# Rotary embedding on one core: the first and last rows as f32 on SyncE's queue, a new order of partitions, and constants copied by a shuffle

## The chip, the core and the metric

One core of a Trainium2 chip runs the whole program. Times are device microseconds (us); lower is better. "Span" is the stretch that the profile covers, from the program's first to its last profiled instruction; the time of an execution is a little longer. GpSimd, SyncE and ScalarE each issue transfers on a queue of their own (q0, q1 and q10 in the pages); the core's 16 DMA engines move them in packets. A transfer has *landed* when all 16 of its completions are in the records. A *drain* is an instruction that waits until its engine's work is done. f32 numbers take 4 bytes, bf16 numbers 2. The verdict "faster" or "slower" needs 2%.

## The reference

Every row of 64 numbers is rotated by an angle that depends on its position in the sequence (0 to 1023) and on the column.

```python
batch, n_heads, seq, head_dim = 8, 8, 1024, 64      # x is f32: 16.8 MB in, 16.8 MB out
angles = np.outer(positions, freqs)                 # freqs has 32 entries
cos, sin = np.cos(angles), np.sin(angles)
out_first  = x_first * cos - x_second * sin
out_second = x_first * sin + x_second * cos
```

## The kernel before

The 64 (batch, head) pairs make 8 tiles of 8 heads. A partition holds a chunk of 64 consecutive rows of one head: 16 KB in f32, 8 KB as bf16 on the chip. GpSimd issues all loads and stores of x and out; they cast between f32 and bf16. ScalarE makes the sines once; VectorE does six multiplies or adds for each tile.

```python
    def hbm(t, g):
        return bass.AP(tensor=t.tensor, offset=t.offset + g * P * run, ap=[[run, P], [1, run]])

    pos_i = singles.tile([P, C, 1], positions.dtype)
    nc.sync.dma_start(                                  # each of 128 partitions reads its 512 B
        out=pos_i,
        in_=bass.AP(tensor=positions.tensor, offset=positions.offset,
                    ap=[[0, group], [C, chunks], [1, C]]))
    fr = singles.tile([P, half], f32)
    nc.scalar.dma_start(out=fr, in_=freqs[None, :].to_broadcast([P, half]))   # 128 x 128 B

    for g in range(ntiles):
        xt = xpool.tile([P, C, d], bf16)
        nc.gpsimd.dma_start(out=xt.rearrange("p c d -> p (c d)"), in_=hbm(x, g))
    # ... turns on VectorE, then sin_h and cos_h on ScalarE (cut) ...
    for g in range(ntiles):
        # ... six operations on VectorE, 128x2048 bf16 each (cut) ...
        nc.gpsimd.dma_start(out=hbm(out, g), in_=ot.rearrange("p c d -> p (c d)"))
```

Of the kernel before, what the change touches and what calls it, by code (L numbers as in the profile page):

```python
# [2 lines left out]

# [4 lines left out]


@with_exitstack  # L10
def kernel(
    ctx: ExitStack,
    tc: tile.TileContext,
    x: bass.AP,
    freqs: bass.AP,
    positions: bass.AP,
    out: bass.AP,
):
    nc = tc.nc
    f32 = mybir.dt.float32  # L20
    bf16 = mybir.dt.bfloat16
    Sin = mybir.ActivationFunctionType.Sin
    Alu = mybir.AluOpType

    b, h, seq, d = x.shape
    bh = b * h
    half = d // 2
    P = 128
    twopi = 2 * math.pi


    C = 64
    chunks = seq // C
    group = P // chunks
    ntiles = bh // group
    run = C * d
    assert chunks * C == seq and group * chunks == P and ntiles * group == bh

    singles = ctx.enter_context(tc.tile_pool(name="singles", bufs=1))
    xpool = ctx.enter_context(tc.tile_pool(name="xin", bufs=ntiles))  # L40
    opool = ctx.enter_context(tc.tile_pool(name="xout", bufs=ntiles))
    tpool = ctx.enter_context(tc.tile_pool(name="tmp", bufs=2))

    def hbm(t, g):
        return bass.AP(tensor=t.tensor, offset=t.offset + g * P * run, ap=[[run, P], [1, run]])


    pos_i = singles.tile([P, C, 1], positions.dtype)
    nc.sync.dma_start(
        out=pos_i,  # L50
        in_=bass.AP(tensor=positions.tensor, offset=positions.offset,
                    ap=[[0, group], [C, chunks], [1, C]]))
    fr = singles.tile([P, half], f32)
    nc.scalar.dma_start(out=fr, in_=freqs[None, :].to_broadcast([P, half]))


    xts = []
    for g in range(ntiles):
        xt = xpool.tile([P, C, d], bf16)
        nc.gpsimd.dma_start(out=xt.rearrange("p c d -> p (c d)"), in_=hbm(x, g))  # L60
        xts.append(xt)


    half_pi = singles.tile([P, 1], f32)
    nc.vector.memset(half_pi, math.pi / 2)  # L65
    pos_f = singles.tile([P, C, 1], f32)
    nc.vector.tensor_copy(out=pos_f, in_=pos_i.bitcast(mybir.dt.int32)[:, :, :1])  # L67
    fturn = singles.tile([P, 1, half], f32)
    nc.vector.tensor_scalar_mul(out=fturn[:, 0, :], in0=fr, scalar1=1.0 / twopi)  # L69
    turns = singles.tile([P, C, half], f32)  # L70
    nc.vector.tensor_mul(out=turns, in0=pos_f.to_broadcast([P, C, half]),  # L71
                         in1=fturn.to_broadcast([P, C, half]))
    whole = singles.tile([P, C, half], f32)
    magic = 1.5 * 2.0 ** 23
    nc.vector.tensor_scalar(out=whole, in0=turns, scalar1=magic, scalar2=magic,  # L75
                            op0=Alu.add, op1=Alu.subtract)
    nc.vector.tensor_sub(out=turns, in0=turns, in1=whole)  # L77
    sin_h = singles.tile([P, C, half], bf16)
    cos_h = singles.tile([P, C, half], bf16)
    nc.scalar.activation(out=sin_h, in_=turns, func=Sin, scale=twopi)  # L80

    nc.scalar.activation(out=whole, in_=turns, func=mybir.ActivationFunctionType.Abs)  # L82
    nc.scalar.activation(out=cos_h, in_=whole, func=Sin, scale=-twopi, bias=half_pi)  # L83

    v = nc.vector
    for g in range(ntiles):
        xt = xts[g]
        xf = xt[:, :, :half]
        xs = xt[:, :, half:]
        ot = opool.tile([P, C, d], bf16)  # L90
        of = ot[:, :, :half]
        os_ = ot[:, :, half:]
        t1 = tpool.tile([P, C, half], bf16)
        t2 = tpool.tile([P, C, half], bf16)
        v.tensor_mul(out=t1, in0=xf, in1=sin_h)  # L95
        v.tensor_mul(out=t2, in0=xs, in1=sin_h)  # L96
        v.tensor_mul(out=of, in0=xf, in1=cos_h)  # L97
        v.tensor_mul(out=os_, in0=xs, in1=cos_h)  # L98
        v.tensor_sub(out=of, in0=of, in1=t2)  # L99
        v.tensor_add(out=os_, in0=os_, in1=t1)  # L100
        nc.gpsimd.dma_start(out=hbm(out, g), in_=ot.rearrange("p c d -> p (c d)"))  # L101


# [1 line left out]
_INS = ['x', 'freqs', 'positions']  # L105
_OUTS = [((8, 8, 1024, 64), 'float32')]


# [23 lines left out]
```

## Time and profile before

| | before |
|---|---|
| time, median of 4 runs | 86.48 us (86.45 to 86.63) |
| profiled run: time, span | 86.43, 84.25 us |
| last load landed (tile 7) | 43.93 us |
| VectorE's last result | 67.7 us |
| last packet / last landing of a store | 82.46 / 82.83 us |
| from the last landing to the end of the span | 1.41 us |

The page of the kernel before: the span; the busy share of two rows in 40 equal slices, in tenths; then for each DMA queue its packets, MB and the share of 16 engines' span.

```profile
span 84.2 us, 132 instructions
DVE 60.7 (72%) x54; ACT 7.0 (8%) x4; POOL 8.9 (11%) x20
...
DVE  0069927999999999999999999999999910000000
...
DMA  0399999999999999999999999999999999999990
...
q0 software_dynamic: 2304, 25.17, 97.2%
q1 hardware_dynamic: 136, 0.07, 0.3%
q10 hardware_dynamic: 144, 0.02, 0.1%
```

The DMA engines are full from the third slice to the last but one. VectorE (DVE) has nothing to do in the last seven slices, so its speed does not matter here. In the packet records an engine moves a row of 16 KB (f32 side) every 0.605 us, in loads and in stores, so 16 engines move 433 GB/s and x and out together need 77.5 us. Only the rest can be won.

The start, in stretches of 0.5 us (stretch, its length, busy us and instructions of VectorE, ScalarE and GpSimd, clock, DMA share, GB/s):

```profile
2.00:2.50 0.50, 0.00 (x0) 0.42 (x1) 0.50 (x2) 1.00 0.20 52
2.50:3.00 0.50, 0.00 (x0) 0.00 (x0) 0.50 (x2) 1.00 0.44 52
3.00:3.50 0.50, 0.00 (x0) 0.00 (x0) 0.50 (x2) 1.00 0.37 38
3.50:4.00 0.50, 0.00 (x0) 0.00 (x0) 0.50 (x3) 1.00 0.44 70
4.00:4.50 0.50, 0.00 (x0) 0.00 (x0) 0.50 (x2) 1.00 0.98 221
```

When all 16 engines are full, they move about 215 GB/s by this count, because a load is counted by its bf16 bytes. Until 4 us there is almost nothing. GpSimd issues its first load at 1.25 us, yet the first sixteen packets of its queue start at 2.8 to 4.5 us.

The end, in SyncE's own waits (who waited for what: total us, times, longest):

```profile
SPq L127 <- DMA out_dram<-ot: 81.2, 4, 66.8
SPq L127 <- PEq L127: 1.0, 2, 0.6
```

SyncE waits for the stores nearly all the time. The last one lands at 82.83 us, and SyncE is through at 83.11; but in the instruction records GpSimd's closing drain ends only at 83.53 us, 0.70 us after the landing, and the closing barriers come after that.

### The profile page before, as it was taken

Reading aid. Unit: us, or ns where it says so; the run is one execution under the profiler, and the core shown is the slowest. Engines: PE = TensorE matmul, PEld = TensorE weight load, DVE = VectorE, ACT = ScalarE, POOL = GpSimd, SP = SyncE. Lnnn points to the kernel's source line nnn. Section 1 sums busy time; section 2 is a strip of 40 time slices with the busy share of each in tenths; the row PEclk is TensorE's granted clock in tenths of the full one; section 3 lists DMA queues with packets and bytes.
Section 4 is the critical chain, followed back from the end, with each engine's and each line's share of the span. In section 5 each row is a group of like instructions: output and inputs, shape, how many; then the busy total and the mean of one; then the engine's idle time right before and its main releaser. Section 6 shows DMA issues by size and latency. Waiting matters only on the chain.

```text
span 84.2 us, 132 instructions
## 1 busy us (share of the span) xinstructions
DVE 60.7 (72%) x54; ACT 7.0 (8%) x4; POOL 8.9 (11%) x20
## 2 busy tenths in 40 slices
DVE  0069927999999999999999999999999910000000
ACT  4100079900000000000000000000000000000000
POOL 5960000000201100200200200100020020000000
DMA  0399999999999999999999999999999999999990
GB/s 2 60 210 214 214 218 218 214 214 214 214 222 210 218 218 210 218 218 214 210 342 405 459 405 467 381 490 381 482 389 467 405 451 420 428 443 405 467 373 0
DMA packets 2584, 25.25 MB, mean 300 GB/s; under 512 B 408, under 2 KB 536, under 8 KB 536
## 3 DMA queue, kind: packets, MB, share of 16 engines
q0 software_dynamic: 2304, 25.17, 97.2%
q1 hardware_dynamic: 136, 0.07, 0.3%
q10 hardware_dynamic: 144, 0.02, 0.1%
HBM read 16.86 MB, written 16.78 MB: 399 GB/s over the span
## 4 chain that ended last, share of the span: by engine, by line
issue 65%; DMA 10%; POOL 4%; POOLq 1%; PEldq 0%
DMA xt<-in_x_dram 10%; POOL out_dram L101 4%; POOLq L127 1%; POOLq L101 0%; PEldq L127 0%
## 5 line engine op out<-in xcount | busy, mean ns | idle before, releaser
L95 DVE TENSOR_TENSOR t<-xt,sin_h 128x2048 bf16<-128x2048 bf16 x8 | 9.8, 1224 | 2.0 <-ACT sin_h L80 2.0
L101 POOL DMA_DIRECT2D out_dram<-ot x8 | 4.3, 535 | 58.6 <-DVE ot L100 58.6
L99 DVE TENSOR_TENSOR ot<-ot,t 128x2048 bf16<-128x2048 bf16 x8 | 9.8, 1225 | 0.0
L97 DVE TENSOR_TENSOR ot<-xt,cos_h 128x2048 bf16<-128x2048 bf16 x8 | 9.8, 1224 | 0.0
L100 DVE TENSOR_TENSOR ot<-ot,t 128x2048 bf16<-128x2048 bf16 x8 | 9.8, 1224 | 0.0
L98 DVE TENSOR_TENSOR ot<-xt,cos_h 128x2048 bf16<-128x2048 bf16 x8 | 9.8, 1223 | 0.0
L96 DVE TENSOR_TENSOR t<-xt,sin_h 128x2048 bf16<-128x2048 bf16 x8 | 9.8, 1223 | 0.0
L60 POOL DMA_DIRECT2D xt<-in_x_dram x8 | 4.4, 578 | 0.8 <-PEq L127 0.8
L67 DVE CAST pos_f<-pos_i 128x64 f32<-128x64 int32 x1 | 0.2, 196 | 4.1 <-DMA pos_i<-in_positions_dram 4.1
L80 ACT ACTIVATE sin_h<-turns 128x2048 bf16<-128x2048 f32 x1 | 1.9, 1911 | 8.7 <-DVE turns L77 8.7
L77 DVE TENSOR_TENSOR turns<-turns,whole 128x2048 f32<-128x2048 f32 x1 | 2.3, 2293 | 0.0
L71 DVE TENSOR_TENSOR turns<-pos_f,fturn 128x2048 f32<-128x2048 f32 x1 | 2.3, 2291 | 0.0
L83 ACT ACTIVATE cos_h<-whole,half_pi 128x2048 bf16<-128x2048 f32 x1 | 2.0, 2003 | 0.0
L82 ACT ACTIVATE whole<-turns 128x2048 f32<-128x2048 f32 x1 | 1.9, 1896 | 0.0
L80 ACT ACT_TABLE_LOAD x1 | 1.3, 1283 | 1.1 <-PEq L116 1.1
L75 DVE TENSOR_SCALAR whole<-turns 128x2048 f32<-128x2048 f32 x1 | 1.2, 1226 | 0.0
L65 DVE MEMSET half_pi<- 128x1 f32 x1 | 0.1, 59 | 0.8 <-PEq L116 0.8
L69 DVE TENSOR_SCALAR fturn<-fr 128x32 f32<-128x32 f32 x1 | 0.2, 174 | 0.0
L116 POOL MEMSET const-float32-0.0<- 128x1 f32 x1 | 0.1, 99 | 0.2 <-issue 0.2
L116 POOL MEMSET const-bfloat16-1.0<- 128x1 bf16 x1 | 0.1, 102 | 0.0
L116 POOL MEMSET const-float32-1.0<- 128x1 f32 x1 | 0.1, 99 | 0.0
L116 POOL MEMSET const-uint8-127<- 128x1 uint8 x1 | 0.1, 99 | 0.0
## 6 DMA issues: line engine op xcount, KB each, us to landing
out_dram<-ot POOLq DMA_DIRECT2D x8, 2048.0 KB, 21.7
xt<-in_x_dram POOLq DMA_DIRECT2D x8, 1024.0 KB, 23.6
pos_i<-in_positions_dram SPq DMA_DIRECT2D x1, 64.0 KB
fr<-in_freqs_dram ACTq DMA_DIRECT2D x1, 16.0 KB, 3.6
```

The lines of the kernel that those rows point to most:

```text
L60: nc.gpsimd.dma_start(out=xt.rearrange("p c d -> p (c d)"), in_=hbm(x, g))
L71: nc.vector.tensor_mul(out=turns, in0=pos_f.to_broadcast([P, C, half]), in1=fturn.to_broadcast([P, C, half]))
L77: nc.vector.tensor_sub(out=turns, in0=turns, in1=whole)
L80: nc.scalar.activation(out=sin_h, in_=turns, func=Sin, scale=twopi)
L83: nc.scalar.activation(out=cos_h, in_=whole, func=Sin, scale=-twopi, bias=half_pi)
L95: v.tensor_mul(out=t1, in0=xf, in1=sin_h)
L96: v.tensor_mul(out=t2, in0=xs, in1=sin_h)
L97: v.tensor_mul(out=of, in0=xf, in1=cos_h)
L98: v.tensor_mul(out=os_, in0=xs, in1=cos_h)
L99: v.tensor_sub(out=of, in0=of, in1=t2)
L100: v.tensor_add(out=os_, in0=os_, in1=t1)
L101: nc.gpsimd.dma_start(out=hbm(out, g), in_=ot.rearrange("p c d -> p (c d)"))
```

## The change

The intent: let SyncE's queue carry f32 rows while GpSimd's queue is not yet, or no longer, the bottleneck, and read less at the start. The first 16 of 64 rows of each partition of tile 0 come in as f32 in two pieces of 8 rows (2 KB runs), and ScalarE casts them. The last 24 rows of tile 7 are computed in f32 and go out on SyncE in three such pieces. A partition now holds chunk p//8 of head p%8, so that one copy of the positions for every 8 partitions and one of the frequencies for every 32 are enough; VectorE's shuffle copies them within groups of 32. SyncE waits for the earlier transfers before the end instead of at the end. Tile 1 is rotated before tile 0.

```diff
+    def hbm(t, g, lo=0, hi=C):
+        return bass.AP(tensor=t.tensor, offset=t.offset + g * P * run + lo * d,
+                       ap=[[run, chunks], [seq * d, group], [1, (hi - lo) * d]])
+    piece = 8
+    head = 2 * piece
+    x0 = singles.tile([P, head, d], f32)
+    for r in range(0, head, piece):
+        nc.sync.dma_start(out=x0[:, r:r + piece], in_=hbm(x, 0, r, r + piece))
+    nc.vector.memset(pos_i, 0)
+    nc.scalar.dma_start(out=pos_i[0:P:group].bitcast(positions.dtype), in_=...)  # 16 rows
+    nc.vector.memset(fr, 0.0)
+    nc.scalar.dma_start(out=fr[0:P:32], in_=freqs[None, :].to_broadcast([P // 32, half]))
     for g in range(ntiles):
+        lo = 0 if g else head
+        nc.gpsimd.dma_start(out=xts[g][:, lo:], in_=hbm(x, g, lo))
+    nc.vector.stream_shuffle(pos_i, pos_i, [i // group * group for i in range(32)])
+    nc.vector.stream_shuffle(fr, fr, [0] * 32)
 ...
+    nc.scalar.copy(out=xts[0][:, :head], in_=x0)
+    tail = 3 * piece
+    for g in [1, 0] + list(range(2, ntiles)):
+        hi = C if g < ntiles - 1 else C - tail
 ...
+    last = singles.tile([P, tail, d], f32)
+    rotate(ntiles - 1, C - tail, C, last)
+    sp.keepalive_nop(ins=[sp.lower_ap(cos_h)])
+    for done in [pos_i, fr, x0] + ots[:-1]:
+        sp.clobber_nop(outs=[sp.lower_ap(done)])       # SyncE waits here, before the end
+    for r in range(0, tail, piece):
+        ... sp.dma_start(out=hbm(out, ntiles - 1, lo, lo + piece), in_=last[:, r:r + piece])
+    sp.clobber_nop(outs=[sp.lower_ap(ots[-1])])
```

More of the change, by code (lines that the diff above doesn't have):

```diff
@@ L42 @@
     tpool = ctx.enter_context(tc.tile_pool(name="tmp", bufs=2))
-    def hbm(t, g):
-        return bass.AP(tensor=t.tensor, offset=t.offset + g * P * run, ap=[[run, P], [1, run]])
-    pos_i = singles.tile([P, C, 1], positions.dtype)
-    nc.sync.dma_start(
-        out=pos_i,
+    def hbm(t, g, lo=0, hi=C):
+        return bass.AP(tensor=t.tensor, offset=t.offset + g * P * run + lo * d,
+                       ap=[[run, chunks], [seq * d, group], [1, (hi - lo) * d]])
+    xts = [xpool.tile([P, C, d], bf16, name="xt") for _ in range(ntiles)]
+    piece = 8
[3 more added lines that the diff above has]
+        nc.sync.dma_start(out=x0[:, r:r + piece], in_=hbm(x, 0, r, r + piece))
+    i32 = mybir.dt.int32
+    words = mybir.dt.size(positions.dtype) // 4
+    pos_i = singles.tile([P, C, words], i32)
+    nc.vector.memset(pos_i, 0)
+    nc.scalar.dma_start(
+        out=pos_i[0:P:group].bitcast(positions.dtype),
         in_=bass.AP(tensor=positions.tensor, offset=positions.offset,
-                    ap=[[0, group], [C, chunks], [1, C]]))
+                    ap=[[C, chunks], [1, C], [1, 1]]))
     fr = singles.tile([P, half], f32)
-    nc.scalar.dma_start(out=fr, in_=freqs[None, :].to_broadcast([P, half]))
-    xts = []
+    nc.vector.memset(fr, 0.0)
+    nc.scalar.dma_start(out=fr[0:P:32], in_=freqs[None, :].to_broadcast([P // 32, half]))
     for g in range(ntiles):
-        xt = xpool.tile([P, C, d], bf16)
-        nc.gpsimd.dma_start(out=xt.rearrange("p c d -> p (c d)"), in_=hbm(x, g))
-        xts.append(xt)
+        lo = 0 if g else head
+        nc.gpsimd.dma_start(out=xts[g][:, lo:], in_=hbm(x, g, lo))
+    nc.vector.stream_shuffle(pos_i, pos_i, [i // group * group for i in range(32)])
+    nc.vector.stream_shuffle(fr, fr, [0] * 32)
     half_pi = singles.tile([P, 1], f32)
@@ L66 @@
     pos_f = singles.tile([P, C, 1], f32)
-    nc.vector.tensor_copy(out=pos_f, in_=pos_i.bitcast(mybir.dt.int32)[:, :, :1])
+    nc.vector.tensor_copy(out=pos_f, in_=pos_i[:, :, :1])
     fturn = singles.tile([P, 1, half], f32)
@@ L83, with rotate @@
     nc.scalar.activation(out=cos_h, in_=whole, func=Sin, scale=-twopi, bias=half_pi)
+    nc.scalar.copy(out=xts[0][:, :head], in_=x0)
     v = nc.vector
-    for g in range(ntiles):
-        xt = xts[g]
-        xf = xt[:, :, :half]
-        xs = xt[:, :, half:]
-        ot = opool.tile([P, C, d], bf16)
+    def rotate(g, lo, hi, ot):
+        xf = xts[g][:, lo:hi, :half]
+        xs = xts[g][:, lo:hi, half:]
         of = ot[:, :, :half]
         os_ = ot[:, :, half:]
-        t1 = tpool.tile([P, C, half], bf16)
-        t2 = tpool.tile([P, C, half], bf16)
-        v.tensor_mul(out=t1, in0=xf, in1=sin_h)
-        v.tensor_mul(out=t2, in0=xs, in1=sin_h)
-        v.tensor_mul(out=of, in0=xf, in1=cos_h)
-        v.tensor_mul(out=os_, in0=xs, in1=cos_h)
+        sin = sin_h[:, lo:hi]
+        cos = cos_h[:, lo:hi]
+        t1 = tpool.tile([P, C, half], bf16, name="t1")[:, :hi - lo]
+        t2 = tpool.tile([P, C, half], bf16, name="t2")[:, :hi - lo]
+        v.tensor_mul(out=t1, in0=xf, in1=sin)
+        v.tensor_mul(out=t2, in0=xs, in1=sin)
+        v.tensor_mul(out=of, in0=xf, in1=cos)
+        v.tensor_mul(out=os_, in0=xs, in1=cos)
         v.tensor_sub(out=of, in0=of, in1=t2)
         v.tensor_add(out=os_, in0=os_, in1=t1)
-        nc.gpsimd.dma_start(out=hbm(out, g), in_=ot.rearrange("p c d -> p (c d)"))
+    tail = 3 * piece
+    ots = []
+    for g in [1, 0] + list(range(2, ntiles)):
+        hi = C if g < ntiles - 1 else C - tail
+        ot = opool.tile([P, C, d], bf16, name="ot")[:, :hi]
+        rotate(g, 0, hi, ot)
+        ots.append(ot)
+        nc.gpsimd.dma_start(out=hbm(out, g, 0, hi), in_=ot)
+    last = singles.tile([P, tail, d], f32)
+    rotate(ntiles - 1, C - tail, C, last)
+    sp = nc.sync
+    sp.keepalive_nop(ins=[sp.lower_ap(cos_h)])
+    for done in [pos_i, fr, x0] + ots[:-1]:
+        sp.clobber_nop(outs=[sp.lower_ap(done)])
+    for r in range(0, tail, piece):
+        lo = C - tail + r
+        tc.keep_in_program_order(
+            sp.dma_start(out=hbm(out, ntiles - 1, lo, lo + piece), in_=last[:, r:r + piece]))
+    sp.clobber_nop(outs=[sp.lower_ap(ots[-1])])
+    for r in range(0, tail - piece, piece):
+        sp.clobber_nop(outs=[sp.lower_ap(last[:, r:r + piece])])
 _INS = ['x', 'freqs', 'positions']
```

## The prediction

> **What bounds the kernel now.** The DMA engines. The page's slices show DMA at 9 (90% or more) from the third slice to the last but one; the software queue takes 97.2% of 16 engines' span. Stretches: loads run at 214 to 216 GB/s counted on the bf16 side (about 430 in f32) from 4 to 43 us, stores at 418 to 440 GB/s until 82 us. VectorE is 72% busy and off the path: a store queued at 22.6 us (timeline) only moves after the loads, at 43 us, and VectorE ends at 68 us, 14 us before the DMA. In the packet records one engine moves a 16 KB f32 row every 0.605 us, so 128 rows cost 77.5 us. The rest, 84.2 - 77.5 = 6.7 us, is start and end; only that can be won.
>
> *Start.* GpSimd issues the first load at 1.25 us; its packets start between 2.8 and 4.5 us; the engines are full from about 4.7 us. From 0 to 4 us the DMA share is 0.18, mostly constants (q1, q10: 0.4% of 16 engines' span; q1's packets of 27 ns, on 8 engines only, sit at 2.2 to 4.5 us, among the first loads).
>
> *End.* The last packet is at 82.4 us, the last landing at 82.83 us. GpSimd's closing drain ends only at 83.53 us, 0.7 us later; closing barriers follow to 84.2. SyncE is through its waits at 83.1 us, so GpSimd's drain sets the end.
>
> **What the change does.**
> 1. 16 of 64 rows of tile 0 (32 KB an engine) leave GpSimd's queue: 2 x 0.605 = 1.21 us of transfer. Issued at 0.74 us on SyncE, they should flow from about 1.8 to 2.3 us (the constants' packets began 1.0 and 1.5 us after their issue), mostly while the engines idle. The Trainium skill ("DMA: Bandwidth & Descriptors", Issuing engines are not separate DMA queues) says all queues share the 16 engines; so this gains only where they idle now. Gain 1.0 to 1.2 us.
> 2. Constants: 128 + 128 rows become about 16 + 4. Gain 0.1 to 0.4 us on the engines that finish last. Two shuffles and two memsets on VectorE (some 0.1 to 0.2 us each): off the path.
> 3. The tail on SyncE: same bytes, so no transfer gain; 24 packets of 2 KB an engine may cost 0.1 to 0.3 us more. But GpSimd's queue finishes about 1 us before the end, so its 0.7 us drain hides, and SyncE's earlier waits are done beforehand: gain 0.5 to 0.6 us.
> 4. f32 outputs of 24 rows put tile 7 on VectorE at about 10 instead of 7 us, the cast of tile 0 about 1 us on ScalarE: within the 14 us of slack.
> 5. The new order of partitions changes the HBM stride; I expect the same 0.605 us.
>
> Sum: about 1.1 + 0.25 + 0.55 - 0.15 = 1.75 us, or a little more, of 86.46.
>
> **Prediction:** 84.6 us, 83.6 to 85.5 in 8 of 10. Faster by over 2% 0.58, within 2% 0.39, slower 0.03.
>
> **What would show each step:** x0 packets between 1.8 and 4 us, tile 0's and tile 1's landings about 1.2 us earlier; loads ending near 41.8 us; SyncE's queue last to land, near 81.4 us; SyncE's drain and not GpSimd's last before the closing barrier, the span ending 0.85 us after the landing rather than 1.4; VectorE ending near 71 to 72 us.
>
> **What would make it wrong:** x0's small packets come so slowly that they collide with GpSimd's first loads; the tail's three issues on SyncE come late and leave the engines idle (they wait for tile 6's landing first); the new stride slows HBM.

## The result

| | before | after |
|---|---|---|
| time, median of 4 runs | 86.48 | 85.36 us (85.36 to 85.53) |
| ratio after / before | | 0.9872 (0.9855 to 0.9889) |
| profiled run: time, span | 86.43, 84.25 | 85.36, 83.58 |
| time outside the span | 2.19 | 1.78 |
| tile 1 landed / tile 7 landed | 14.67 / 43.93 | 13.96 / 43.24 |
| tile 6 stored: 15 engines / the last | 77.97 / 77.98 | 77.26 / 77.77 |
| last landing | 82.83 | 82.69 |
| last landing to end of span | 1.41 | 0.89 |

A ratio is the mean time of one kernel's fast runs over that of the other's fast runs of the same rounds, so it is not quite the ratio of the medians. The change is 1.3% faster: within 2%, and inside the range that was predicted, but the gain is 1.1 us where 1.75 or a little more was summed.

The page after, the lines that answer to those of before:

```profile
span 83.6 us, 163 instructions
DVE 63.5 (76%) x66; ACT 9.3 (11%) x6; POOL 8.7 (10%) x20
...
DVE  1024995089999999999999999999999999920000
...
DMA  0899999999999999999999999999999999999992
...
q0 software_dynamic: 2304, 24.12, 94.2%
q1 hardware_dynamic: 720, 1.31, 5.1%
q10 hardware_dynamic: 40, 0.01, 0.0%
q14 instruction: 1, 0.01, 0.0%
```

The last line is new: one packet that fetches instructions. It becomes important. The start after:

```profile
2.00:2.50 0.50, 0.00 (x0) 0.00 (x0) 0.50 (x2) 1.00 0.51 102
2.50:3.00 0.50, 0.00 (x0) 0.00 (x0) 0.50 (x2) 1.00 0.91 156
3.00:3.50 0.50, 0.00 (x0) 0.00 (x0) 0.50 (x2) 1.00 0.77 140
3.50:4.00 0.50, 0.00 (x0) 0.00 (x0) 0.50 (x2) 1.00 1.26 325
4.00:4.50 0.50, 0.00 (x0) 0.00 (x0) 0.50 (x2) 1.00 1.09 223
```

The engines are busy 1.5 us earlier than before, yet the loads land only 0.7 us earlier. SyncE's waits after, and its issue of the tail (start, length, what):

```profile
SPq L137 <- DMA out_dram<-ot: 56.7, 7, 27.1
...
SPq L144 <- DMA out_dram<-last: 1.9, 2, 1.3
...
SPq L170 <- DMA out_dram<-last: 0.5, 1, 0.5
```

```profile
77.84 2.27 SPq L141 DMA_DIRECT2D out_dram<-last  x3
```

At the end only one wait, for the last piece, is left. GpSimd's drain ends at 81.50 us, before the last landing, and SyncE's at 82.83.

The difference of the two profiled runs, 1.07 us, in parts: the start -0.71 (tile 1, tile 7 and 15 of 16 engines at tile 6 all agree within 0.02 us); from there to the last landing 0.57 is given back (-0.71 becomes -0.14); the closing part -0.52; the time outside the span -0.41.

**A measure used below.** *Lag* at time t is t minus the time that the bytes of x and out moved by then would take at 433 GB/s (packet records, f32 side: a bf16 load packet counts twice). Constants do not count. A smaller lag is better; where lag grows, the engines lose time there.

| kernel | lag at 5 | 12 | 40 | 44 | 77 us | last landing | closing | outside |
|---|---|---|---|---|---|---|---|---|
| before | 4.24 | 4.40 | 4.56 | 4.67 | 4.78 | 82.83 | 1.41 | 2.19 |
| after | 3.28 | 3.64 | 3.80 | 3.91 | 4.10 | 82.69 | 0.89 | 1.78 |
| e1 head only | 3.55 | 4.37 | 4.53 | 4.55 | 4.66 | 82.93 | 1.42 | 2.21 |
| e2 order and constants only | 3.16 | 3.31 | 3.51 | 4.63 | 4.78 | 83.18 | 1.42 | 1.78 |
| e3 tail only | 4.46 | 4.62 | 4.78 | 4.81 | 4.95 | 83.54 | 0.86 | 1.77 |
| e4 after, 8 early rows | 3.39 | 3.51 | 3.68 | 3.99 | 4.18 | 82.67 | 0.88 | 1.80 |
| e5 before, 8 memsets | 4.42 | 4.57 | 4.74 | 4.75 | 4.91 | 83.54 | 1.41 | 1.77 |
| e6 after, 46 memsets | 3.26 | 3.62 | 3.81 | 3.90 | 4.05 | 82.45 | 0.88 | 1.79 |
| e7 after, no early rows | 3.29 | 3.40 | 3.56 | 4.60 | 4.75 | 83.39 | 0.85 | 1.78 |
| e8 after, no tail | 3.31 | 3.59 | 3.75 | 3.83 | 4.01 | 82.36 | 1.43 | 1.79 |
| e9 order only | 3.89 | 4.10 | 4.26 | 4.54 | 4.65 | 82.76 | 1.42 | 2.20 |
| e10 constants only, old order | 3.82 | 3.92 | 4.08 | 4.37 | 4.54 | 83.04 | 1.44 | 1.77 |
| e11 e10 with the tail | 3.83 | 3.92 | 4.08 | 4.32 | 4.49 | 83.10 | 0.89 | 1.78 |
| e12 e11, 46 memsets | 3.85 | 3.95 | 4.14 | 4.25 | 4.38 | 82.50 | 0.89 | 1.78 |

One trace for each kernel; e3 and e5 start exactly as before does, and their lag at 12 us (4.62, 4.57) against 4.40 shows how far that number moves with the same transfers at the start. It moved less with small constants: the three traces with 16 early rows have 3.59 to 3.64. Times of the experiments are medians; their ratios are against before on the same chip.

### The profile page after: what moved, and what is told of

It reads as the page before. It is cut to its first block, busy times and chain, and to the rows that moved or that the text cites. A ratio compares the mean times of both kernels' runs of the same rounds, so it can differ in the third digit from the quotient of the medians.

```text
span 83.6 us, 163 instructions
## 1 busy us (share of the span) xinstructions
DVE 63.5 (76%) x66; ACT 9.3 (11%) x6; POOL 8.7 (10%) x20
## 4 chain that ended last, share of the span: by engine, by line
DVE 67%; DMA 12%; ACT 7%; DVEq 1%; SPq 1%; issue 0%; ACTq 0%
DMA x<-in_x_dram 12%; DVE t L114 11%; DVE t L115 11%; DVE ot L119 10%; DVE ot L117 10%; DVE ot L116 10%; DVE ot L118 10%; ACT sin_h L96 2%; ACT L96 2%; ACT L101 2%; ACT xt L101 1%; DVEq L170 1%; DVE last L117 1%; DVE last L118 1%; DVE last L116 1%; SPq L56 1%
## 5 line engine op out<-in xcount | busy, mean ns | idle before, releaser
L114 DVE TENSOR_TENSOR t<-xt,sin_h 128x2048 bf16<-128x2048 bf16 (+2 forms) x9 | 9.9, 1099 | 3.5 <-ACT sin_h L96 3.5
L115 DVE TENSOR_TENSOR t<-xt,sin_h 128x2048 bf16<-128x2048 bf16 (+2 forms) x9 | 9.9, 1099 | 0.0
L117 DVE TENSOR_TENSOR ot<-xt,cos_h 128x2048 bf16<-128x2048 bf16 (+1 forms) x8 | 9.3, 1167 | 0.0
L119 DVE TENSOR_TENSOR ot<-ot,t 128x2048 bf16<-128x2048 bf16 (+1 forms) x8 | 9.3, 1167 | 0.0
L116 DVE TENSOR_TENSOR ot<-xt,cos_h 128x2048 bf16<-128x2048 bf16 (+1 forms) x8 | 9.3, 1166 | 0.0
L118 DVE TENSOR_TENSOR ot<-ot,t 128x2048 bf16<-128x2048 bf16 (+1 forms) x8 | 9.3, 1166 | 0.0
L101 ACT CAST xt<-x 128x1024 bf16<-128x1024 f32 x1 | 1.0, 1045 | 0.0
L117 DVE TENSOR_TENSOR last<-xt,cos_h 128x768 f32<-128x768 bf16 x1 | 0.9, 950 | 0.0
L119 DVE TENSOR_TENSOR last<-last,t 128x768 f32<-128x768 f32 x1 | 0.9, 950 | 0.0
L116 DVE TENSOR_TENSOR last<-xt,cos_h 128x768 f32<-128x768 bf16 x1 | 0.9, 949 | 0.0
```

Source lines behind the costliest of these rows:

```text
L101: nc.scalar.copy(out=xts[0][:, :head], in_=x0)
L114: v.tensor_mul(out=t1, in0=xf, in1=sin)
L115: v.tensor_mul(out=t2, in0=xs, in1=sin)
L116: v.tensor_mul(out=of, in0=xf, in1=cos)
L117: v.tensor_mul(out=os_, in0=xs, in1=cos)
L118: v.tensor_sub(out=of, in0=of, in1=t2)
```

## The experiments

All twelve gave correct results. They ran in three jobs (e1 to e4, e5 to e8, e9 to e12), each on a chip of its own; the kernel before took 86.51 to 86.56 us (medians) there. The whole change ran beside none of them, so it is compared with them by the ratios to before. All twelve are within 2% of before.

**e1: the early rows alone** (order and broadcast constants as before; positions move to ScalarE's queue).

```diff
-    nc.sync.dma_start(out=pos_i, ...)
+    for r in range(0, 16, 8):
+        nc.sync.dma_start(out=x0[:, r:r + 8], in_=hbm(x, 0, r, r + 8))
+    nc.scalar.dma_start(out=pos_i, ...)
```

> The kernel before with the early f32 rows of tile 0 alone (the positions move to ScalarE's queue, constants stay broadcast). In the pair of traces the loads of tiles 1 to 7 land 0.69 to 0.76 us earlier with the whole change. Theory A (the head gives what the first 256 KB, 0.6 us of transfer, fill of the idle start; the second 256 KB only displaces GpSimd's loads): landings of the loads 0.3 to 0.6 us earlier than before, second x0 piece landing only after 10 us, time 86.0 to 86.3. Theory B (all 512 KB count, 1.2 us): landings 1.0 us or more earlier, time 85.3 to 85.6.

86.73 us, ratio 1.0018 (0.9982 to 1.0053; one of six runs was slow and is left out). Both theories were wrong: no gain at all. The lag is 0.7 us better than before at 5 us and as before at 12 us. The issues show what happened (queue, operation, count, KB each, us from issue to landing):

```profile
xt<-in_x_dram POOLq DMA_DIRECT2D x1, 768.0 KB, 8.4
x<-in_x_dram SPq DMA_DIRECT2D x2, 256.0 KB, 5.7
pos_i<-in_positions_dram ACTq DMA_DIRECT2D x1, 64.0 KB
fr<-in_freqs_dram ACTq DMA_DIRECT2D x1, 16.0 KB, 10.3
```

The frequencies' 128 small packets now take 10.3 us to land instead of 3.6: they run among the load packets, at 6.5 to 11.3 us. Filling the start with rows pushed the constants into the loads. That this is what the gain was lost to is my reading: the packets alone are busy for 2.4 us, 0.15 us for each engine, and the rest of the loss is a lower DMA share from 5 to 12 us (0.98 instead of 1.04). The frequencies were also issued later (1.96 us instead of 0.74), behind the positions on ScalarE's queue; no run has that move alone.

**e2: the order of partitions and the shuffled constants alone** (positions stay on SyncE).

```diff
-    ap=[[run, P], [1, run]]
+    ap=[[run, chunks], [seq * d, group], [1, run]]
-    # 128 rows of positions, 128 of freqs
+    # 16 rows of positions, 4 of freqs, two shuffles
```

> The kernel before with the partition order and the shuffled constants alone. 73 KB less and 240 packets less at the start: landings of the loads 0.1 to 0.3 us earlier, time 86.2 to 86.4. If the new partition order slowed HBM, the period of a 16 KB row on one engine would rise above 0.605 us and the time above 86.5. If the instruction packet (queue 14) that lies inside the span after the change goes with the number of VectorE's or ScalarE's instructions, it is inside here too (VectorE has 5 instructions more than before); if it goes with SyncE's, it is not.

86.42 us, ratio 0.9987 (0.9961 to 1.0013). The time is near what was expected, and for a wrong reason. The start is far better than expected: tile 1 lands at 13.59 us, 1.08 earlier than before, and the lag at 12 us, 3.31, is better than that of the whole change. GpSimd's first sixteen packets start at 2.61 to 2.96 us instead of 2.8 to 4.5, 1.33 us after the issue. So what had kept the start idle was not GpSimd but the many small packets of the constants, together with the old order (e9 and e10 part the two). But between 40 and 44 us the lag grows by 1.12 us: the gain is given back there.

**e3: the tail alone.**

```diff
-    # tile 7: 64 rows as bf16 on GpSimd's queue
+    # tile 7: 40 rows as before; 24 rows as f32 in three pieces on SyncE, with its earlier waits
```

> The kernel before with the f32 tail on SyncE and its earlier waits alone. My theory: the closing part after the last landing falls from 1.41 to 0.86 us (GpSimd's drain hidden), the last landing itself stays within 0.3 us of 82.83 us or comes later, because 2 KB packets cost 80 ns instead of 75.6 and the engines end the tail apart: span 83.6 to 84.2. Rival: the tail itself brings the last landing forward by 0.3 us or more. If the 8 KB instruction packet moves into the span with the tail (6 VectorE and 13 SyncE instructions more), one engine will be 0.5 us behind from there on, and the time outside the span falls from 2.2 to 1.8 us.

86.15 us, ratio 0.9962 (0.9927 to 0.9997); span 84.40 us, above the expected range. The closing part falls to 0.86 us as I said. The last landing does not come forward: tile 6 is stored at 78.10 us on all engines but one and the last at 78.61, and then the last piece lands at 83.54. The instruction packet is inside the span (58.7 us), and the time outside falls to 1.77 us.

**e4: 8 instead of 16 early rows** in the whole change.

```diff
-    head = 2 * piece
+    head = piece
```

> The kernel after with 8 instead of 16 early rows: one piece on SyncE. Theory A (second piece runs between 5 and 11 us among GpSimd's packets, fills no idle time and costs about 0.3 us there): loads land as early as after or up to 0.3 us earlier, time 85.1 to 85.4. Theory B (each piece fills idle time): loads land 0.5 us later than after, time 85.8 to 86.0.

85.36 us, ratio 0.9864 (0.9841 to 0.9886), indistinguishable from the whole change: tile 1 lands at 13.82 us, 0.14 earlier than with 16 rows. The second piece of 256 KB is worth nothing at the start. In the whole change it lands at 11.46 us, its 2 KB packets alternating with GpSimd's rows: 128 of them, eight for each engine if they are spread evenly, start between 5.0 and 10.4 us, one every 0.68 us or so, which is a row and a packet (0.605 + 0.080).

**e5: the kernel before with eight empty memsets on VectorE.**

```diff
+    pad = singles.tile([P, 1], f32)
+    for _ in range(8):
+        nc.vector.memset(pad, 0.0)
```

> The kernel before with 8 empty memsets of one column on VectorE in its idle start; nothing else. In the traces so far the 8 KB instruction packet lies after the span where VectorE has 61 instructions in the trace (before, e1) and inside it, at VectorE's 49th to 51st instruction, where it has 67 or more (after, e2, e3, e4). If VectorE's count is the cause: the packet comes inside the span at about 58 us, the time outside the span falls from 2.2 to 1.8 us, and one engine's landings lag the others by about 0.5 us from there on; time 86.2 to 86.6, as before (0.4 us off outside, up to 0.4 us on inside). If the cause is the tail or the shuffles themselves: packet after the span, 2.2 us outside, time as before.

86.85 us, ratio 1.0027 (0.9986 to 1.0068). The first theory holds, though the packet came at 52.1 us, not at 58, and the median is above the expected 86.2 to 86.6 (its six runs spread from 86.36 to 87.31). Its page has the line that only the whole change had:

```profile
q14 instruction: 1, 0.01, 0.0%
```

It starts at the 51st of VectorE's recorded instructions (the 49th to 51st in the traces before), the time outside the span is 1.77 us, and one engine's last landing is 0.60 us behind the others (83.54 against 82.94). Nothing else was changed. So a longer instruction stream on VectorE moves one fetch of instructions from after the span into it: 0.4 us less outside, 0.6 us more for one DMA engine inside. No change of the time is seen.

**e6: the whole change with 46 such memsets** before VectorE's first wait.

```diff
+    for _ in range(46):
+        tc.keep_in_program_order(nc.vector.memset(pad, 0.0))
+    # the two shuffles are kept in program order behind them
```

> The kernel after with 46 such memsets on VectorE before it first waits, so that its 50th instruction, and with it the instruction packet, falls into the idle start (3 to 5 us) and not into the stores. If the packet is what puts one engine 0.5 us behind: no lagging engine in the landings of the stores, tile 6 lands at about 77.3 us and not 77.8, last landing 82.1 to 82.5 instead of 82.69, still 1.8 us outside the span, time 84.8 to 85.2. If the lag has another cause: lag as before, time 85.3 to 85.5.

85.16 us, ratio 0.9836 (0.9808 to 0.9865). The packet came at 17.9 us, at VectorE's 62nd instruction, not in the idle start; that was a miss. One engine is 0.48 us late at tile 2's landing (19.32 against 18.84) and no longer at tile 3's, and no engine lags in the stores: tile 6 is stored at 77.28 us on all engines (77.77 in the whole change) and the last landing is 82.45 instead of 82.69. The span is 0.25 us shorter. It is the fastest kernel measured here; the whole change was not run beside it on that chip, and the intervals of the two ratios overlap slightly.

**e7: the whole change without the early rows.**

```diff
-    for r in range(0, head, piece):
-        nc.sync.dma_start(out=x0[:, r:r + piece], in_=hbm(x, 0, r, r + piece))
-        nc.gpsimd.dma_start(out=xts[g][:, lo:], in_=hbm(x, g, lo))
+        nc.gpsimd.dma_start(out=xts[g][:, 0:], in_=hbm(x, g))
```

> The kernel after without the early f32 rows (constants and tail as after). From e1 (head alone gains nothing by 12 us) and e2 (constants alone gain more by 10 us than the whole change) I expect that the head is worth nothing or costs: loads of tiles 1 to 6 land 0.2 to 0.4 us earlier than after. If the stall of about 1 us that e2 shows between 40 and 43 us belongs to the partition order, it comes here too and the time is 85.6 to 86.0; without it 84.9 to 85.3. Rival (head is worth its 1.2 us or half of it): loads land 0.3 us or more later than after, time above 85.7 without a stall.

86.03 us, ratio 0.9929 (0.9899 to 0.9959). At the start the early rows cost: without them tile 1 lands at 13.81 us, 0.15 earlier, and GpSimd's first packets start at 2.61 to 2.95 us; with them only at 3.50 to 4.02. But the stall of e2 is back: the lag grows by 1.04 us between 40 and 44 us. The same stretches in e7 and then in e6, which has the early rows (columns as above):

```profile
39.00:40.00 1.00, 1.00 (x2) 0.00 (x0) 0.00 (x0) 1.00 1.22 254
40.00:41.00 1.00, 1.00 (x2) 0.00 (x0) 0.00 (x0) 1.00 1.12 147
41.00:41.50 0.50, 0.50 (x1) 0.00 (x0) 0.00 (x0) 1.00 1.17 131
41.50:42.00 0.50, 0.50 (x2) 0.00 (x0) 0.00 (x0) 1.00 1.14 131
42.00:42.50 0.50, 0.50 (x1) 0.00 (x0) 0.00 (x0) 1.00 0.25 49
```

```profile
39.00:40.00 1.00, 1.00 (x2) 0.00 (x0) 0.00 (x0) 1.00 0.94 197
40.00:41.00 1.00, 1.00 (x2) 0.00 (x0) 0.00 (x0) 1.00 1.02 213
41.00:41.50 0.50, 0.50 (x2) 0.00 (x0) 0.00 (x0) 1.00 1.23 229
41.50:42.00 0.50, 0.50 (x1) 0.00 (x0) 0.00 (x0) 1.00 0.79 164
42.00:42.50 0.50, 0.50 (x2) 0.00 (x0) 0.00 (x0) 1.00 1.03 279
```

The DMA share of e7 stays above 1 while only 131 to 147 GB/s move: packets that usually take 0.625 us take up to 1.3. This is in the last load packets, before any store has moved. The early rows are worth 0.5 us of time by the ratios and 0.7 by the medians and the last landings (82.69 against 83.39), all of it because this stall is small with them.

**e8: the whole change without the tail.**

```diff
-    # 24 rows of tile 7 on SyncE
+    nc.gpsimd.dma_start(out=hbm(out, g), in_=ot)
```

> The kernel after without the tail: all of tile 7 goes by GpSimd. Closing part 1.41 us again instead of 0.86. If the tail's own transfers cost what the closing part gains: last landing 0.3 to 0.5 us earlier than after's 82.69, time within 0.2 us of after (85.2 to 85.6). If the tail is a net gain of about 0.5 us: time 85.8 to 86.0.

85.75 us, ratio 0.9904 (0.9876 to 0.9932), between the two expectations. The last landing comes 0.33 us earlier than in the whole change, the closing part is 1.43 us again (0.54 longer). The tail is a net gain of 0.2 us in the span and about 0.3% of the time; the intervals of the two ratios overlap a little.

**e9: the new order alone**, constants broadcast.

```diff
-    ap=[[run, P], [1, run]]                            # x and out
+    ap=[[run, chunks], [seq * d, group], [1, run]]
-    ap=[[0, group], [C, chunks], [1, C]]               # positions
+    ap=[[C, chunks], [0, group], [1, C]]
```

> The kernel before with the new order of partitions alone; constants broadcast as before. Its start should be as before (GpSimd's first packets spread over 2.8 to 4.6 us). If the order of partitions is what stalls all engines between 40 and 43 us in e2 and e7: a stall of about 1 us here too, time 87.2 to 87.8. If the stall needs the early start with it (or comes from the small constants): no stall over 0.3 us, time 86.3 to 86.7.

86.37 us, ratio 0.9974 (0.9951 to 0.9996). No large stall (the lag grows by 0.28 us): the order alone does not make it. And the start is not as before, which I had not expected: the lag at 12 us is 4.10. The positions' queue has 144 packets instead of 136: 128 rows and one completion for each of 16 engines, where it was 8. With the chunks outermost instead of the 8 zero-stride copies, the load is spread over all engines. The Trainium skill says this ("DMA: Bandwidth & Descriptors", Why a DMA increments its semaphore by 16 and not by 1: the number of engines divides the slowest dimensions of both sides), and this trace agrees.

**e10: shuffled constants alone, in the old order** (64 rows of positions in four transfers, 4 of frequencies).

```diff
+    for q in range(0, P, 32):
+        (nc.scalar if q == 96 else nc.sync).dma_start(out=pos_i[q:q + chunks]..., in_=...)
+    nc.vector.stream_shuffle(pos_i, pos_i, [i % chunks for i in range(32)])
```

> The kernel before with shuffled constants alone, in the old order of partitions (64 rows of positions in four transfers, 4 rows of freqs, instead of 128 and 128). If the many small packets of the broadcast constants are what hold GpSimd's first packets back: their first packets on all 16 engines between 2.6 and 3.3 us instead of 2.8 to 4.5, loads landing 0.8 to 1.1 us earlier than before. If the stall between 40 and 43 us goes with the order: none here, loads of tile 7 land near 42.9 us, last landing 81.9 to 82.3 with one engine 0.4 to 0.5 us late for the instruction packet, time 85.3 to 85.7. If it goes with the early start: stall here too, time 86.3 to 86.6.

86.21 us, ratio 0.9953 (0.9933 to 0.9974). Less than half of what I expected, and a time between the two that I had named: GpSimd's first packets start at 2.62 to 3.62 us, the lag at 12 us is 3.92, tile 1 lands 0.35 us earlier than before, and the lag grows by 0.29 us between 40 and 44 us. So constants and order help the start together (e2: 3.31), and the stall is not the order's alone.

**e11 and e12: e10 with the tail, and then with the 46 memsets.**

```diff
+    # e11: tail as in the change     # e12: also 46 memsets before VectorE's first wait
```

> e10 with the tail on SyncE. From e8 against e4 and the change the tail is worth 0.3 to 0.5 us: time 84.8 to 85.4 without a stall, 85.9 to 86.2 with one.

> e11 with the 46 memsets of e6, which there took the lag of one engine away and 0.2 us of time: 0.1 to 0.4 us less than e11, 84.5 to 85.1 without a stall.

85.71 us, ratio 0.9895 (0.9874 to 0.9915), and 85.53 us, ratio 0.9877 (0.9848 to 0.9907). The medians differ by 0.18 us as expected, but the intervals overlap widely (e12's six runs spread from 85.17 to 85.86), so this gain of the memsets is not shown. No engine lags in e12's stores (tile 6 at 77.48 and 77.54 us), and the packet came at 16.5 us. Both are slower than I had expected; their lag at 12 us, 3.92 and 3.95, is that of e10. With no early rows and the old order, e12 is as fast as the whole change by its ratio.

## Why the prediction was right, and where its sum was not

The time is inside the predicted range, 0.14 us from its upper end, and partly by luck: "faster by over 2%" had been held the likeliest outcome and did not come; the instruction fetch, which nobody forecast, took 0.41 us off outside the span for 0.24 inside; and the early rows pay in a way that was not predicted (they keep a stall away). Of the signs that were named, the span's end came as said (0.89 us after the landing, 0.85 forecast); the early rows' packets run on to 10.4 us instead of 4, tile 1 is 0.71 us earlier instead of 1.2, the loads end at 43.2 instead of 41.8, and SyncE's last landing is at 82.69 instead of 81.4. Five points in order:

1. **The early rows, "Gain 1.0 to 1.2 us": wrong as a step.** The argument was that they fill time in which the engines idle. It saw correctly that all queues share the 16 engines (the page cited above; here, with early rows GpSimd's first packets are held back from 2.6 to 3.5 us, e7 against after). But it took the idle time as given, while the same change removes its cause: with the small constants GpSimd's queue starts at 2.6 us, and 512 KB issued from 0.74 us on, whose first packet moves at 2.19 us, find almost nothing idle to fill. Alone, with broadcast constants, they gain nothing (e1); within the change they cost 0.24 us of lag by 12 us (3.64 against 3.40 in e7). The prediction had named this as a risk: small packets that collide with GpSimd's first loads. The Trainium skill ("DMA: Bandwidth & Descriptors", Queues, rings and completion order) says that an engine changes queues at packets; the second piece landing at 11.46 us, between GpSimd's rows, agrees.
2. **The constants, "0.1 to 0.4 us": mis-sized.** I summed the busy time of their packets, 0.4% of the engines. (They were not "mostly" what ran before 4 us either: in the records they are 3.4 of 11.8 us of busy time.) What they cost was the delay of the loads behind them: with the new order, tile 1 lands 1.08 us earlier (e2). Point 1 and point 2 both bid for the same idle second; the sum counted it twice. Together they give 0.71, not 1.35 us.
3. **The tail, gain 0.5 to 0.6 against a cost of 0.1 to 0.3: right in mechanism.** The closing part shrinks by 0.52 us and GpSimd's drain is no longer last. The cost was at the upper end: in e6, where no engine lags, tile 7 takes 5.17 us from tile 6's landing, against 4.85 before. Packets of 2 KB follow each other every 80 ns instead of 75.6 (24 of them: 0.11 us); the rest I only see, as single packets of up to 0.24 us.
4. **Slack: right.** VectorE ends at 73.7 us, 2 us later than I said: its first product of positions and frequencies starts at 7.78 us instead of 5.25, and ScalarE, which cast tile 0 first and loaded a table before and after the cast (1.28 us each), began the sines at 15.18 us although their input was ready at 13.66. It costs nothing here: SyncE issues the tail only at 77.84 us.
5. **The new order leaves 0.605 us for a row: right** for loads and stores in their middle.

Two things were not in the sum. The instruction packet, moved into the span by VectorE's longer stream (shown by e5), takes 0.41 us from the time outside the span and makes one engine 0.5 us late at tile 6; at the last landing that is 0.24 us (after against e6). So the sum reads: start -0.71, tail +0.33, late engine +0.24, closing -0.52, outside -0.41: -1.07 us.

**Left open.** Between 40 and 44 us the engines mostly lose more when the loads run earlier: 0.01 to 0.11 us at a lag of 4.5 to 4.8 (before, e1, e3, e5), 0.11 to 0.29 at 4.1 to 4.3 (e9 to e12), 1.04 and 1.12 at 3.5 to 3.6 (e2, e7). With early rows it is only 0.08 to 0.11 at 3.8 (after, e6, e8) and 0.31 with half of them (e4). It comes at the same time of the run, about 41 us, in the last load packets. That it is small with the early rows is shown by e7; how, and what it is, no run shows. The early rows also make the loads 0.24 us later, and that alone may be the reason: no run delays the loads without them. This is where a gain of 1 us at the start goes when it is won without them.

## What to carry to other kernels

Two remedies for one idle stretch do not add: ask first what keeps the stretch idle, and remove that alone before filling it. Small broadcast transfers at the start are not priced by their bytes or their busy time but by the large transfers that wait behind them; read one copy and spread it on the chip, with a wide outermost dimension. After any change, check the late landings of every single DMA engine and the time outside the span, since both can move with the mere number of instructions.

## What the Trainium skill lacked or had wrong

- "Runtime: NRT & Kernel Launch", Instruction fetch mechanics, calls the fetch of the next block "mostly hidden". It does run on a queue of its own as the page says (q14 here), but the page does not tell that it takes a DMA engine's time: when it fell into the stores, the packet of 8 KB left one DMA engine 0.5 to 0.6 us late (after, e5), and whether it falls inside the span changed the time outside from 2.2 to 1.8 us. The page gives blocks of 16 KiB; the packet recorded here is of 8 KB.
- "DMA: Bandwidth & Descriptors", Rules for kernel authors, tells of issue costs and sizes, but no page says that small hardware-queue loads delay the first packets of GpSimd's queue: 2.8 to 4.5 us with broadcast constants, 2.61 to 2.96 us without and in the new order (e2), 2.62 to 3.62 us without and in the old one (e10).
- No page has the end of a kernel whose last store is on GpSimd's queue: its drain ended 0.70 us after the last landing, and the span 1.41 us after it; with SyncE's queue last, 0.85 to 0.89 us.
- No page has the loss of 1.0 to 1.1 us in the last loads (e2, e7), whose cause stays open here.
